# Feed-forward products of a streaming encoder on one core: a step's 512-column products ahead of its 256-column ones, operands laid at other places in SBUF

## The chip, the cores and the metric

One core of one Trainium2 chip runs the kernel. The metric is the device time of one execution in microseconds (us). Three runs of the kernel before lie between 1232.41 and 1232.6 us, with a median of 1232.55 us.

## What is computed

The reference is a two-layer encoder on 256 tokens of width 1024. Each layer is a half-step feed-forward (SwiGLU of width 2816), a mixer of three branches with one input and one output projection, a cross-attention to 256 memory tokens, and a second half-step feed-forward. The part that the change touches:

```python
def swiglu(h, w1, w3, w2):
    return (jax.nn.silu(h @ w1) * (h @ w3)) @ w2

for l in range(DEPTH):                                   # DEPTH = 2
    x = x + 0.5 * swiglu(rms_norm(x, ffn1_norm_g[l]), ffn1_w1[l], ffn1_w3[l], ffn1_w2[l])
    ...                                                  # mixer, cross-attention
    x = x + 0.5 * swiglu(rms_norm(x, ffn2_norm_g[l]), ffn2_w1[l], ffn2_w3[l], ffn2_w2[l])
return rms_norm(x, final_norm_g)
```

All arrays are float32. D_MODEL is 1024 (8 blocks of 128, KD), D_FF is 2816 (22 blocks of 128, KF).

## The kernel before

**Two parts of every number.** TensorE multiplies in the type fp32r. Each float32 operand is held as a hi part, rounded to fp32r, and a lo part, what the rounding left. A product of two such operands is hi x hi + hi x lo + lo x hi. For the weights, ScalarE makes the hi part (`w_hi`, line 127) and VectorE the lo part (`w_lo`, line 128) from the float32 weights `w_raw`, which SP's DMA queue brings (line 100).

**Feed-forward.** The activations lie with features on the partitions: `xn` is the input, 8 blocks of 128 features, and `g` the hidden one, 22 blocks. For block k, `x[:, k]` is a [128, 2, 256] piece: the hi parts of 256 tokens and their lo parts. `mm_w` makes a block's share with two products. The first loads 128 columns of `w_hi` as the array's stationary weights and streams all 512 columns of `x[:, k]`, hi and lo, into a PSUM bank of 512 columns. The second loads the same slice of `w_lo` and streams the 256 hi columns alone into the bank's second half. So 512- and 256-column products alternate. `gemm_w` takes a *step* of weights from `W` (`W.take`): up to 4 blocks by 256 output columns, and works it into two banks (m = 0 and 1, 128 output columns each), 4 blocks each. For w1 and w3 a bank is two steps of 4; for w2 it is five steps of 4 and one of 2. `gemm_both` does the same for the very first 256 columns of w1 and w3 together, whose steps are shorter. ScalarE and VectorE then add a bank's halves (`f_p`, `f_t`), and make `g` of them.

The last feed-forward's w2 (`final`), and half of the mixer's input projection, go through `gemm_x`, where the roles are exchanged: the activations are the stationary operand and 512 columns of weights stream. The other projections go through `gemm_n`: three products of 256 columns with weights as the stationary operand.

**The order of work.** The Tile framework orders each engine's instructions from a simulated timeline and from priorities. Weights are split up to three steps ahead (`SPLIT_AHEAD`), into three buffers each of `w_hi` and `w_lo`; a buffer is free when the last product that reads it is done.

**Where the operands lie.** The tables `XN_AT`, `G_AT` and `W_AT` shift a tile's contents by a number of float32 elements (4 bytes each) inside a slightly larger tile. The built program places `xn`'s tile 64 bytes past a multiple of 256 bytes of a partition, `g`'s tile 160 bytes, and the `w_hi` and `w_lo` tiles 128 bytes, in both kernels. While one product streams, the weights of the next are loaded. In this text the *distance* of a product is the start of its streaming operand minus the start of the weights that are loaded meanwhile, modulo 256 bytes. In the kernel before it is, by these tables:

| Products | streaming operand at | weights loaded meanwhile at | distance |
|---|---|---|---|
| `gemm_w`, `xn` | 64 + 4x8 = 96 | 128 + 4x16 = 192 | 160 |
| `gemm_w`, `g` | 160 + 4x48 = 352, so 96 | 192 | 160 |
| `gemm_x` (weights stream), `xn` | 128 + 4x56 = 352, so 96 | 96 | 0 |
| `gemm_x`, last w2 with `g` | 128 + 4x48 = 320, so 64 | 160 + 4x40 = 320, so 64 | 0 |
| `gemm_n`, `xn` of mixer and attention | 96 | 128 + 4x48 = 320, so 64 | 32 |

All blocks and slices are multiples of 256 bytes apart, so a distance holds for all products of a kind.

Of the kernel before, what the change touches and what calls it, by code (L numbers as in the profile page):

```python
# [9 lines left out]
F32R = mybir.dt.float32r  # L10
# [5 lines left out]
P = 128  # L16
D = 1024
S = 256
KD = D // P
# [5 lines left out]
CW = 256  # L25
# [5 lines left out]
PART_BUFS = 3  # L31
# [2 lines left out]
QE_BUFS = 1  # L34
T3_BUFS = 8
PAD = {"xn": 16, "g": 128, "mix": 0}
XN_AT = {"ffn1": 8, "mix": 8, "xattn": 8, "ffn2": 8}

W_AT = {("w13", False): 16, ("w1", False): 16, ("w3", False): 16, ("w2", False): 16, ("w2", True): 48,
        ("in", True): 56, ("kv", False): 40, ("kv", True): 48, ("out", False): 0, ("o", False): 0, "other": 48}  # L40
G_AT = (48, 40)
MIX_AT = 0
Q_AT, P_AT = 56, 8
X_LOADS = ((0, 1), (1, 1), (2, 2), (4, 2), (6, 2))
# [18 lines left out]
class Weights:  # L63
# [45 lines left out]
    def _split(self):  # L109
        nc, i = self.nc, self.n_split  # L110
        self.n_split += 1
        u, unit, at, nk = self.steps[i]
        while self.n_load < len(self.pieces) and self.pieces[self.n_load][0] <= u:
            self._load()
        at_ = W_AT.get((unit.key, unit.beside), W_AT["other"])
        hi = self.pool.tile([P, 4 * CW + 64], F32R, name="w_hi", tag="w_hi", bufs=PART_BUFS)[:, at_:at_ + 4 * CW]
        lo = self.pool.tile([P, 4 * CW + 64], F32R, name="w_lo", tag="w_lo", bufs=PART_BUFS)[:, at_:at_ + 4 * CW]
        if unit.key == "w13":
            hi, lo = (t[:, 0:2 * nk * CW].rearrange("p (h k c) -> p h k c", h=2, k=nk) for t in (hi, lo))
            t = self._both(u, at).rearrange("p (h k c) -> p h k c", h=2, k=nk)  # L120
        elif unit.beside:
            hi, lo = (t.rearrange("p (h k c) -> p h k c", h=2, k=2)[:, :, 0:nk, :] for t in (hi, lo))
            t = self.raw[u].rearrange("p h (k c) -> p h k c", k=4)[:, :, at:at + nk, :]
        else:
            hi, lo = (t.rearrange("p (k c) -> p k c", k=4)[:, 0:nk, :] for t in (hi, lo))
            t = self.raw[u].rearrange("p h (k c) -> p h k c", k=4)[:, at, 0:nk, :]
        self.last = nc.scalar.copy(hi, t)  # L127
        nc.vector.tensor_tensor(out=lo, in0=t, in1=hi.bitcast(F32), op=ALU.subtract)  # L128
        self.parts[i] = (hi, lo)
# [88 lines left out]
def trunk(ctx: ExitStack, tc: tile.TileContext, a: dict, out: bass.AP, stop=None, dbg=None):  # L218
# [9 lines left out]
    class Bank:  # L228
# [28 lines left out]
            self.mm(acc, lh, rl, False, False)  # L257
            self.mm(acc, ll, rh, False, stop)

        def mm_w(self, wh, wl, x, begin, stop):  # L260

            self.mm(self.ap, wh, x, begin, stop)
            self.mm(self.ap[:, 1, :], wl, x[:, 0, :], False, stop)

    class Act:

# [22 lines left out]

    def placed(pool, name, k, at, **kw):  # L290

        n = k * 2 * S
        return pool.tile([P, n + PAD[name]], F32R, name=name, bufs=1, **kw)[:, at:at + n].rearrange(
            "p (k u s) -> p k u s", k=k, u=2)

    def mm_bank(split=None):
        return Bank("mm", split)
# [31 lines left out]
    vec_off, n = {}, 0  # L329
# [36 lines left out]
    def gemm_w(key, nk, x, banks):  # L366

        k0 = 0
        while k0 < nk:
            wh, wl, n = W.take(key)  # L370
            for m, bank in enumerate(banks):
                for k in range(n):
                    sl = slice(m * P, (m + 1) * P)
                    bank.mm_w(wh[:, k, sl], wl[:, k, sl], x[:, k0 + k], k0 + k == 0, k0 + k == nk - 1)
            k0 += n
            yield

    def gemm_both(x, pairs):

        k0 = 0  # L380
        while k0 < KD:
            wh, wl, n = W.take("w13")
            for u, banks in enumerate(pairs):
                for m, bank in enumerate(banks):
                    for k in range(n):
                        sl = slice(m * P, (m + 1) * P)
                        bank.mm_w(wh[:, u, k, sl], wl[:, u, k, sl], x[:, k0 + k], k0 + k == 0, k0 + k == KD - 1)
            k0 += n

    def gemm_x(key, nk, x, banks):  # L390
# [36 lines left out]
    class Norm:  # L427


        def __init__(self, l, name, mem=False):  # L430
            self.gains = col(l, name)
            if not mem:
                self.x = placed(keep, "xn", KD, XN_AT[name.split("_")[0]], tag="xn")
            self.ssq = small.tile([P, S], F32, name="ssq", tag="ssq", bufs=2)
# [38 lines left out]
    def ffn(l, f, nrm, nxt, last=False, setup=None):  # L473
        with tc.tile_pool(name="ffn", bufs=2) as fp:
            g = placed(fp, "g", KF, G_AT[last])
            if setup is not None:
                setup = setup(fp)

            for c in range(0, KF, 2):
                t = [fp.tile([P, 2, S], F32, name="f_t", bufs=3) for _ in range(2)]  # L480
                both = l == c == 0 and f == "ffn1"
                if both:
                    pairs = [[mm_bank(2) for _ in range(2)] for _ in range(2)]
                    gemm_both(nrm.x, pairs)
                for u, key in enumerate(("w1", "w3")):
                    if both:
                        banks = pairs[u]
                    else:
                        banks = [mm_bank(2) for _ in range(2)]
                        run(gemm_w(key, KD, nrm.x, banks))  # L490
                    for m in range(2):

                        p = fp.tile([P, S], F32, name="f_p", bufs=3)
                        nc.scalar.copy(p, banks[m][:, 1, :])  # L494
                        nc.vector.tensor_tensor(out=t[m][:, u, :], in0=banks[m][:, 0, :], in1=p, op=ALU.add)  # L495
                if both:
                    first_norm()
                for m in range(2):
                    nc.vector.tensor_tensor(out=t[m], in0=t[m], in1=nrm.R[:, None, :].to_broadcast([P, 2, S]),  # L499
                                            op=ALU.mult)  # L500
                    s = fp.tile([P, S], F32, name="f_s", bufs=2)
                    act(SILU, out=s, in_=t[m][:, 0, :], func=AF.Silu)
                    nc.vector.tensor_tensor(out=s, in0=s, in1=t[m][:, 1, :], op=ALU.mult)
                    hi, lo = split(g[:, c + m, 0, :], g[:, c + m, 1, :], s)
                if setup is not None:

                    with tc.issue_after(hi.ins), tc.issue_after(lo.ins):
                        next(setup, None)
# [3 lines left out]
            for c in range(0, KD, 2):  # L512
                banks = [mm_bank(2) for _ in range(2)]
                run(gemm_w("w2", KF, g, banks))
                for m in range(2):
                    add_tile(c + m, [banks[m][:, u, :] for u in range(2)], 0.5, nxt)
# [183 lines left out]
    def mixer(l, nrm, nxt, mp, kvp):  # L700
        R, rc = nrm.R, nrm.rc
        mix = placed(mp, "mix", KD, MIX_AT)

        def tokens_out(tok, j, gain):
# [472 lines left out]
    for l in range(DEPTH):  # L1177
# [6 lines left out]
        with tc.tile_pool(name="kvp", bufs=1) as kvp, tc.tile_pool(name="mix", bufs=T4_BUFS) as mp:  # L1184
            nxt = Norm(l, "xattn_norm_g")
            k = mixer(l, nrm, nxt, mp, kvp)
# [104 lines left out]
```

## Time and profile before

| What | Value |
|---|---|
| Median of three runs | 1232.55 us |
| Profiled execution, its own time | 1232.48 us |
| Its span, first to last instruction | 1230.7 us |
| TensorE busy (matmuls) | 1221.3 us, 99% of the span |
| VectorE, ScalarE busy | 936.0 us (76%), 738.1 us (60%) |
[...]

Of the profiled execution's 1232.48 us, 1.78 us lie outside the span. Matmuls are pipelined, so the duration of one overlaps the next, and a busy TensorE says little: what counts is the time from the start of one product to the start of the next, called its *pitch* here. It is read from the start times of the timeline, which prints hundredths of a microsecond and merges equal instructions that follow each other into one row with their count.

### The profile page before, as it was taken

How to read it: one execution, taken by the hardware profiler on the slowest of the kernel's cores; microseconds unless marked ns; L12 is line 12 of the kernel's file. 1: busy time of each engine (PE TensorE's matmuls, PEld its weight loads, DVE VectorE, ACT ScalarE, POOL GpSimd, SP SyncE). 2: the span in 40 equal slices, each digit the busy share in tenths (PEclk: the TensorE clock that was granted, in tenths of full speed). 3: DMA queues.
4: the chain of work that ended last, by engine and by line, in shares of the span. 5: the costliest groups of instructions: out<-in, count | busy, mean ns of one | idle time of the engine just before them, and what ended most of it. 6: DMA issues, size and time to landing. Idle time of an engine off the chain costs nothing.

```text
span 1230.7 us, 21670 instructions
## 1 busy us (share of the span) xinstructions
PE 1221.3 (99%) x8378; PEld 1101.4 (89%) x8378; DVE 936.0 (76%) x1649; ACT 738.1 (60%) x1309; POOL 30.5 (2%) x54
## 2 busy tenths in 40 slices
PE   9999999999999999999999999999999999999997
PEld 8888889988999988888888888899898999888886
DVE  7989866888777687776678886679787767778754
ACT  6666645556765665664466654465677646656643
POOL 1000000000100000000000000000000000000000
PEclk9999999999999999999999999999999999999999
DMA  7645555443344355455555455544433534555453
GB/s 264 242 181 192 174 189 200 146 163 138 137 173 171 123 185 201 176 205 188 189 216 204 177 200 188 189 171 158 153 138 145 197 138 155 193 184 200 177 188 120
DMA packets 62569, 219.32 MB, mean 178 GB/s; under 512 B 6913, under 2 KB 8193, under 8 KB 62209
## 3 DMA queue, kind: packets, MB, share of 16 engines
q1 hardware_dynamic: 60976, 213.35, 47.6%
q0 software_dynamic: 768, 3.86, 0.8%
q8 instruction: 66, 1.08, 0.3%
q10 hardware_dynamic: 720, 0.72, 0.2%
q14 instruction: 39, 0.31, 0.1%
HBM read 216.85 MB, written 1.05 MB: 177 GB/s over the span
## 4 chain that ended last, share of the span: by engine, by line
PE 95%; DVE 2%; ACT 1%; issue 1%; DMA 0%; POOLq 0%; POOL 0%; SPq 0%; DVEq 0%; ACTq 0%
PE mm L244 88%; PE aux L244 2%; PE aux L834 1%; DVE w_lo L128 0%; PE aux L832 0%; DMA w_raw<-in_weights_dram 0%; ACT w_hi L127 0%; PE mm L242 0%; PE aux L242 0%; PE aux L827 0%; PE aux L984 0%; PE aux L913 0%; PE aux L1105 0%; PE aux L970 0%; DVE qe L815 0%
## 5 line engine op out<-in xcount | busy, mean ns | idle before, releaser
L128 DVE TENSOR_TENSOR w_lo<-w_raw,w_hi 128x1024 fp32r<-128x1024 f32 (+1 forms) x411 | 494.3, 1205 | 212.5 <-ACT w_hi L127 207.4
L127 ACT CAST w_hi<-w_raw 128x1024 fp32r<-128x1024 f32 (+1 forms) x411 | 425.0, 1035 | 361.0 <-PE mm L244 219.3
L244 PE MATMUL mm<-xn,w_hi 128*128 128x512 f32 (+1 forms) x2028 | 601.2, 359 | 0.6 <-DVE xn L362 0.5
L244 PE MATMUL mm<-xn,w_lo 128*128 128x256 f32 x1728 | 476.7, 280 | 0.0
L244 PEld LDWEIGHTS mm<-xn,w_hi 128*128 128x128 f32 x2028 | 357.7, 188 | 56.3 <-DVE xn L362 0.7
L244 PEld LDWEIGHTS mm<-xn,w_lo 128*128 128x128 f32 x1728 | 324.6, 188 | 3.6
L244 PE MATMUL mm<-g,w_hi 128*128 128x512 f32 x528 | 180.8, 392 | 0.0
L244 PE MATMUL mm<-g,w_lo 128*128 128x256 f32 x528 | 141.8, 280 | 0.0
L244 PEld LDWEIGHTS mm<-g,w_hi 128*128 128x128 f32 x528 | 96.5, 188 | 19.0
L244 PEld LDWEIGHTS mm<-g,w_lo 128*128 128x128 f32 x528 | 99.3, 188 | 2.9
L244 PE MATMUL mm<-w_hi,xn 128*128 128x512 f32 (+1 forms) x318 | 89.1, 374 | 0.0
L494 ACT COPY f_p<-mm 128x256 f32<-128x256 f32 x176 | 63.9, 365 | 24.5 <-PE mm L244 23.8
L495 DVE TENSOR_TENSOR f_t<-mm,f_p 128x256 f32<-128x256 f32 x176 | 73.0, 418 | 2.5 <-ACT f_p L494 2.4
L244 PEld LDWEIGHTS mm<-w_hi,xn 128*128 128x128 f32 x318 | 57.2, 188 | 9.2
L499 DVE TENSOR_TENSOR f_t<-f_t,R 128x512 f32<-128x512 f32 x88 | 60.2, 688 | 1.9 <-ACT R L463 0.7
L244 PE MATMUL mm<-w_lo,xn 128*128 128x512 f32 (+1 forms) x160 | 56.6, 378 | 1.0 <-DVE w_lo L128 1.0
L244 PE MATMUL mm<-w_hi,g 128*128 128x512 f32 x176 | 51.9, 390 | 0.0
L244 PE MATMUL mm<-mem_n,w_hi 128*128 128x256 f32 x248 | 46.7, 284 | 0.0
L244 PE MATMUL mm<-o,w_hi 128*128 128x256 f32 x248 | 46.2, 281 | 0.0
L467 DVE SCALAR_TENSOR_TENSOR xT<-mm,xT 128x256 f32<-128x256 f32 x80 | 32.0, 419 | 17.3 <-PE mm L244 17.3
L244 PE MATMUL mm<-mix,w_hi 128*128 128x256 f32 x256 | 44.7, 279 | 0.0
L244 PE MATMUL mm<-w_hi,mem_n 128*128 128x512 f32 x128 | 39.5, 393 | 0.0
(253 smaller groups left out, 1476.6 us busy)
## 6 DMA issues: line engine op xcount, KB each, us to landing
w_raw<-in_weights_dram SPq DMA_DIRECT2D x395, 512.0 KB, 4.0
w_raw<-in_weights_dram SPq DMA_DIRECT2D x18, 256.0 KB, 3.6
m_t<-in_mem_t_dram POOLq DMA_DIRECT2D x2, 1024.0 KB, 6.4
xT<-in_x_t_dram SPq DMA_DIRECT2D x3, 256.0 KB, 6.0
cst<-in_c_cst_dram POOLq DMA_DIRECT2D x1, 696.0 KB, 4.5
out_dram<-yg SPq DMA_DIRECT2D x2, 320.0 KB, 2.5
gw<-in_gates_w_dram POOLq DMA_DIRECT2D x2, 256.0 KB, 6.8
fg<-in_final_norm_g_dram POOLq DMA_DIRECT2D x1, 512.0 KB, 5.7
```

Source lines behind the costliest of these rows:

```text
L127: self.last = nc.scalar.copy(hi, t)
L128: nc.vector.tensor_tensor(out=lo, in0=t, in1=hi.bitcast(F32), op=ALU.subtract)
L244: i = self.last = nc.tensor.matmul(acc, lhsT, rhs, start=begin, stop=stop, skip_group_check=True)
L467: nc.vector.scalar_tensor_tensor(out=xT[:, j, :], in0=h, scalar=scale, in1=xT[:, j, :], op0=ALU.mult, op1=ALU.add)
L494: nc.scalar.copy(p, banks[m][:, 1, :])
L495: nc.vector.tensor_tensor(out=t[m][:, u, :], in0=banks[m][:, 0, :], in1=p, op=ALU.add)
L499: nc.vector.tensor_tensor(out=t[m], in0=t[m], in1=nrm.R[:, None, :].to_broadcast([P, 2, S]), op=ALU.mult)
L834: nc.tensor.matmul(sb[bs, i, :], ke[:, 1 + i, cb], qe[:, 1 + i, cb], start=True, stop=True, skip_group_check=True)
```

## The change

Four things change, all in the feed-forward:

- `xn` and `g` hold all hi parts of all blocks, then all lo parts. A block's 512 columns are then two pieces of 256, 8 KB apart in `xn` and 22 KB apart in `g`.
- `mm_w` gets a whole step's products for a bank, and issues the 512-column ones of all its blocks first, then the 256-column ones.
- `XN_AT` and `G_AT` put `xn` at 64 and `g` at 64 (modulo 256 bytes). `W_AT` has one place for hi and one for lo weights: hi at 64, lo at 32. The distance is 0 while hi weights are loaded and 32 while lo weights are loaded.
- The mixer, the attention and the last w2 keep their places, and their order of products.

```diff
-XN_AT = {"ffn1": 8, "mix": 8, "xattn": 8, "ffn2": 8}
-
-W_AT = {("w13", False): 16, ("w1", False): 16, ("w3", False): 16, ("w2", False): 16, ("w2", True): 48,
...
-G_AT = (48, 40)
+XN_AT = {"ffn1": 0, "mix": 8, "xattn": 8, "ffn2": 0}
+
+W_FF = (48, 40)
+W_AT = {("w13", False): W_FF, ("w1", False): W_FF, ("w3", False): W_FF, ("w2", False): W_FF, ("w2", True): (48, 48),
...
+G_AT = (40, 40)
...
-        def mm_w(self, wh, wl, x, begin, stop):
-
-            self.mm(self.ap, wh, x, begin, stop)
-            self.mm(self.ap[:, 1, :], wl, x[:, 0, :], False, stop)
+        def mm_w(self, steps):
+
+
+            for wh, _, x, begin, stop in steps:
+                self.mm(self.ap, wh, x, begin, stop)
+            for _, wl, x, _, stop in steps:
+                self.mm(self.ap[:, 1, :], wl, x[:, 0, :], False, stop)
...
-        return pool.tile([P, n + PAD[name]], F32R, name=name, bufs=1, **kw)[:, at:at + n].rearrange(
-            "p (k u s) -> p k u s", k=k, u=2)
+        t = pool.tile([P, n + PAD[name]], F32R, name=name, bufs=1, **kw)[:, at:at + n]
+        return t.rearrange("p (k u s) -> p k u s" if name == "mix" else "p (u k s) -> p k u s", k=k, u=2)
...
             for m, bank in enumerate(banks):
-                for k in range(n):
-                    sl = slice(m * P, (m + 1) * P)
-                    bank.mm_w(wh[:, k, sl], wl[:, k, sl], x[:, k0 + k], k0 + k == 0, k0 + k == nk - 1)
+                sl = slice(m * P, (m + 1) * P)
+                bank.mm_w([(wh[:, k, sl], wl[:, k, sl], x[:, k0 + k], k0 + k == 0, k0 + k == nk - 1)
+                           for k in range(n)])
```

What this does to TensorE's order is seen in the first layer's first feed-forward, at w1's and w3's second 256 columns. `mm_372` and `mm_373` are the two banks; the numbers behind `w_hi` and `w_lo` tell one step from the next. Before, at the change from one step to the next:

```order
L244 MATMUL mm_373<-xn_126,w_hi_326 128x512
L244 MATMUL mm_373<-xn_126,w_lo_327 128x256
L244 MATMUL mm_372<-xn_126,w_hi_346 128x512
L244 MATMUL mm_373<-xn_126,w_hi_346 128x512
L244 MATMUL mm_372<-xn_126,w_lo_347 128x256
L244 MATMUL mm_372<-xn_126,w_hi_346 128x512
```

Now, over the same two steps:

```order
L246 MATMUL mm_373<-xn_126,w_hi_326 128x512 x4
L246 MATMUL mm_373<-xn_126,w_lo_327 128x256 x4
L246 MATMUL mm_372<-xn_126,w_hi_346 128x512 x4
L246 MATMUL mm_372<-xn_126,w_lo_347 128x256 x4
L246 MATMUL mm_373<-xn_126,w_hi_346 128x512 x4
L246 MATMUL mm_373<-xn_126,w_lo_347 128x256 x4
```

A hi and a lo product no longer take turns: four hi products follow each other, then four lo products, and a bank's share of a step has one change of kind in either direction instead of four. The scheduler sometimes mixes two banks. This is w2 of the same feed-forward, now, at the end of the first two banks (`mm_1606`, `mm_1607`) and the start of the next two (`mm_1741`, `mm_1742`):

```order
L246 MATMUL mm_1606<-g_161,w_hi_1674 128x512 x2
L246 MATMUL mm_1606<-g_161,w_lo_1675 128x256 x2
L246 MATMUL mm_1607<-g_161,w_hi_1674 128x512 x2
L246 MATMUL mm_1607<-g_161,w_lo_1675 128x256 x2
L246 MATMUL mm_1741<-g_161,w_hi_1697 128x512 x4
L246 MATMUL mm_1742<-g_161,w_hi_1697 128x512 x2
L246 MATMUL mm_1741<-g_161,w_lo_1698 128x256 x4
```

Here w2's last step of two blocks gives runs of two, and the next step's first run is six long, since two of the second bank's hi products come ahead of the first bank's lo products.

VectorE and ScalarE issue the same instructions in nearly the same order. SP's and POOL's orders are as before. This is VectorE in the same feed-forward, before, over one group of 256 hidden columns (`f_t` and `f_s` lead from the banks to `g`; `m_t` and `mem_n` belong to the attention's memory):

```order
L128 TENSOR_TENSOR w_lo<-w_raw,w_hi 128x1024
L495 TENSOR_TENSOR f_t<-mm,f_p 128x256
L503 TENSOR_TENSOR f_s<-f_s,f_t 128x256
L499 TENSOR_TENSOR f_t<-f_t,R 128x512
L128 TENSOR_TENSOR w_lo<-w_raw,w_hi 128x1024
L359 TENSOR_TENSOR g<-f_s,g 128x256
L495 TENSOR_TENSOR f_t<-mm,f_p 128x256
L503 TENSOR_TENSOR f_s<-f_s,f_t 128x256
L128 TENSOR_TENSOR w_lo<-w_raw,w_hi 128x1024
```

And now:

```order
L130 TENSOR_TENSOR w_lo<-w_raw,w_hi 128x1024
L501 TENSOR_TENSOR f_t<-mm,f_p 128x256
L509 TENSOR_TENSOR f_s<-f_s,f_t 128x256
L505 TENSOR_TENSOR f_t<-f_t,R 128x512
L130 TENSOR_TENSOR w_lo<-w_raw,w_hi 128x1024
L365 TENSOR_TENSOR g<-f_s,g 128x256
L509 TENSOR_TENSOR f_s<-f_s,f_t 128x256
L501 TENSOR_TENSOR f_t<-mm,f_p 128x256
L130 TENSOR_TENSOR w_lo<-w_raw,w_hi 128x1024
```

One `f_s` and one `f_t` have changed places; the lo weights stand where they stood.

## Rows read from the trace of the kernel before

**Rows 1.** The page: span, then each engine's busy us, share and instructions.

```profile
span 1230.7 us, 21670 instructions
PE 1221.3 (99%) x8378; PEld 1101.4 (89%) x8378; DVE 936.0 (76%) x1649; ACT 738.1 (60%) x1309; POOL 30.5 (2%) x54
```

**Rows 2.** The chain that ended last: shares by engine; one piece, start, us, products.

```profile
PE 95%; DVE 2%; ACT 1%; issue 1%; DMA 0%; POOLq 0%; POOL 0%; SPq 0%; DVEq 0%; ACTq 0%
...
450.86 175.55 PE mm L244 x1012
```

**Rows 3.** Matmuls by line and shape, whole span: count, busy us, mean ns, idle before.

```profile
L244 PE MATMUL mm<-xn,w_hi 128*128 128x512 f32 x1408 | 486.9, 393 | 0.6 <-DVE xn L362 0.5
L244 PE MATMUL mm<-g,w_hi 128*128 128x512 f32 x528 | 180.8, 392 | 0.0
```

**Rows 4.** Timeline of TensorE, first feed-forward: start us, us, instruction.

```profile
104.34 0.39 PE L244 MATMUL mm<-xn,w_hi 128*128 128x512 f32 x1
104.57 0.28 PE L244 MATMUL mm<-xn,w_lo 128*128 128x256 f32 x1
104.69 0.39 PE L244 MATMUL mm<-xn,w_hi 128*128 128x512 f32 x1
```

**Rows 5.** Timeline of TensorE in the last w2, 512 columns; first and last of a run.

```profile
1175.90 0.39 PE L244 MATMUL mm<-w_lo,g 128*128 128x512 f32 x1
...
1180.43 1.07 PE L244 MATMUL mm<-w_hi,g 128*128 128x512 f32 x4
```

**Rows 6.** Timeline of TensorE in w_out, 256 columns; first and last of a run.

```profile
352.78 0.39 PE L244 MATMUL mm<-mix,w_hi 128*128 128x256 f32 x2
...
355.93 0.28 PE L244 MATMUL mm<-mix,w_hi 128*128 128x256 f32 x1
```

**Rows 7.** Timeline of TensorE in the mixer, from 256 columns to 512.

```profile
216.14 0.28 PE L244 MATMUL mm<-xn,w_lo 128*128 128x256 f32 x1
216.25 0.63 PE L244 MATMUL mm<-w_hi,xn 128*128 128x512 f32 x2
216.72 0.39 PE L244 MATMUL mm<-w_lo,xn 128*128 128x512 f32 x1
216.95 0.63 PE L244 MATMUL mm<-w_hi,xn 128*128 128x512 f32 x2
```

**Rows 8.** The same, at a memory projection.

```profile
326.55 0.63 PE L244 MATMUL mm<-w_hi,mem_n 128*128 128x512 f32 x2
...
327.24 0.39 PE L244 MATMUL mm<-w_hi,mem_n 128*128 128x512 f32 x1
```

**Rows 9.** Timeline of TensorE in the mixer, from 512 columns to 256.

```profile
227.63 0.40 PE L244 MATMUL mm<-w_lo,xn 128*128 128x512 f32 x1
227.87 0.28 PE L244 MATMUL mm<-xn,w_lo 128*128 128x256 f32 x1
227.99 0.40 PE L244 MATMUL mm<-xn,w_hi 128*128 128x256 f32 x2
228.22 0.28 PE L244 MATMUL mm<-xn,w_lo 128*128 128x256 f32 x1
```

**Rows 10.** Timeline of TensorE at the start, four 512-column products of the feed-forward together.

```profile
10.43 1.09 PE L244 MATMUL mm<-xn,w_hi 128*128 128x512 f32 x4
11.36 0.28 PE L244 MATMUL mm<-xn,w_lo 128*128 128x256 f32 x1
```

**Rows 11.** Busy time by engine, 80 to 130 us: PE, PEld, DVE, ACT, POOL; clock, DMA.

```profile
80.00:130.00 50.00, 50.00 (x290) 44.02 (x289) 45.59 (x87) 34.74 (x65) 0.00 (x0) 1.00 0.52 186
```

**Rows 12.** Waits: TensorE over the whole span; then all from 80 to 130 us.

```profile
PE mm L244 <- DVE w_lo L128: 1.0, 2, 0.5
PE mm L244 <- DVE xn L362: 0.5, 1, 0.5
...
ACT w_hi L127 <- PE mm L244: 6.3, 8, 1.2
...
DVE w_lo L128 <- ACT w_hi L127: 4.4, 11, 0.7
```

More of the change, by code (lines that the diff above doesn't have):

```diff
@@ L36 @@
 PAD = {"xn": 16, "g": 128, "mix": 0}
-XN_AT = {"ffn1": 8, "mix": 8, "xattn": 8, "ffn2": 8}
-W_AT = {("w13", False): 16, ("w1", False): 16, ("w3", False): 16, ("w2", False): 16, ("w2", True): 48,
-        ("in", True): 56, ("kv", False): 40, ("kv", True): 48, ("out", False): 0, ("o", False): 0, "other": 48}
-G_AT = (48, 40)
+XN_AT = {"ffn1": 0, "mix": 8, "xattn": 8, "ffn2": 0}
+W_FF = (48, 40)
+W_AT = {("w13", False): W_FF, ("w1", False): W_FF, ("w3", False): W_FF, ("w2", False): W_FF, ("w2", True): (48, 48),
+        ("in", True): (56, 56), ("kv", False): (40, 40), ("kv", True): (48, 48), ("out", False): (0, 0),
+        ("o", False): (0, 0), "other": (48, 48)}
+G_AT = (40, 40)
 MIX_AT = 0
@@ L115, in _split @@
         at_ = W_AT.get((unit.key, unit.beside), W_AT["other"])
-        hi = self.pool.tile([P, 4 * CW + 64], F32R, name="w_hi", tag="w_hi", bufs=PART_BUFS)[:, at_:at_ + 4 * CW]
-        lo = self.pool.tile([P, 4 * CW + 64], F32R, name="w_lo", tag="w_lo", bufs=PART_BUFS)[:, at_:at_ + 4 * CW]
+        hi = self.pool.tile([P, 4 * CW + 64], F32R, name="w_hi", tag="w_hi", bufs=PART_BUFS)[:, at_[0]:at_[0] + 4 * CW]
+        lo = self.pool.tile([P, 4 * CW + 64], F32R, name="w_lo", tag="w_lo", bufs=PART_BUFS)[:, at_[1]:at_[1] + 4 * CW]
         if unit.key == "w13":
@@ L384, in gemm_both @@
                 for m, bank in enumerate(banks):
-                    for k in range(n):
-                        sl = slice(m * P, (m + 1) * P)
-                        bank.mm_w(wh[:, u, k, sl], wl[:, u, k, sl], x[:, k0 + k], k0 + k == 0, k0 + k == KD - 1)
+                    sl = slice(m * P, (m + 1) * P)
+                    bank.mm_w([(wh[:, u, k, sl], wl[:, u, k, sl], x[:, k0 + k], k0 + k == 0, k0 + k == KD - 1)
+                               for k in range(n)])
             k0 += n
```

## The prediction, made before the changed kernel was run

> **What bounds the kernel now.** I read the page first. TensorE is busy for 99% of the span [rows 1], and the chain of waits that ended last runs through it for 95%, in pieces as long as 175.55 us with no other engine between [rows 2]. The next question is whether anybody makes TensorE wait. Its own waits name 1.0 us for `w_lo` and 0.5 us for `xn`, over the whole span [rows 12], so nearly nothing outside TensorE can be won back. VectorE is the nearest follower: in a feed-forward stretch it works 45.59 of 50 us [rows 11]. The time is therefore the number of products times their pitch, and the change leaves the number alone. It has to be judged by pitch.
>
> The feed-forwards hold 1408 + 528 = 1936 pairs of a 512- and a 256-column product [rows 3]. The long piece of the chain is 506 such pairs in 175.55 us: 0.3469 us a pair [rows 2]. The timeline splits it into 0.23 us from a hi product to the lo product behind it and 0.12 us from there to the next hi product [rows 4]. Four pairs, a bank's share of a step, take 4 x 0.3469 = 1.3876 us. [...]
>
> **The change part by part.** *Removed and added.* No instruction is removed or added; products, weight loads, transfers and splits stay as many and as large. What moves is which product follows which, and the distances.
>
> *The settled pitch at the new distances.* The kernel already runs both. In the last w2, 512 columns at distance 0: 20 products from 1175.90 to 1180.43 us, 0.2265 us each [rows 5]. That run also streams two pieces of 256 columns, so the second piece costs nothing visible. In w_out, 256 columns at distance 32: 27 products from 352.78 to 355.93 us, 0.1167 us each [rows 6]. If every product of the feed-forward had these pitches, four pairs would take 4 x (0.2265 + 0.1167) = 1.3728 us, 0.0148 us less than now.
>
> *The price of changing kind.* These runs are long. After the change a run is four products, and then the kind changes. The mixer shows such changes, and there the distances are the ones of the new kernel on both sides: its 512-column products have distance 0, its 256-column ones 32, the last 256 before a 512 has 0, and the last 512 before a 256 has 32. From 256 to 512 the first three products behind the change take 216.95 - 216.25 = 0.70 us [rows 7], or 327.24 - 326.55 = 0.69 us [rows 8]; there are six such changes, three of either kind, so I take 0.694 us. Three settled products would take 0.680 us. The last 256 ahead of the change takes 216.25 - 216.14 = 0.11 us [rows 7]. From 512 to 256, the last 512-column product takes 227.87 - 227.63 = 0.24 us, with 0.235 within the rounding, and the next three of 256 take 228.22 - 227.87 = 0.35 us [rows 9]; there are three changes of this kind at distance 32, all alike. So neither end of a run has the settled pitch: the first products are slower, and the last 512 is slower by 0.009 us.
>
> *The sum for four pairs.* 0.694 (first three of 512) + 0.235 (the fourth) + 0.352 (three of 256) + 0.1125 (the fourth) = 1.3935 us, against 1.3876 now: +0.0059 us. There are 1936 / 4 = 484 such groups: +2.9 us. I take this value, since it is made of products in exactly the new neighbourhoods, while the settled runs are not.
>
> *Its bounds.* Below: all products settled, -0.0148 x 484 = -7.2 us. Above: the nearest row for four grouped hi products of the feed-forward itself is at the start, at the old distance: 11.36 - 10.43 = 0.93 us for four [rows 10]. With 0.235 instead of a fourth of that for the last, and with the fourth 256-column product at the 0.1167 of a settled one, four pairs take 0.6975 + 0.235 + 0.352 + 0.1167 = 1.4012 us, +0.0136, or +6.6 us.
>
> [...]
>
> *The order of the other engines.* Costed at nothing. A step's first lo product now stands behind four hi products instead of one, so the lo weights are wanted 3 x 0.23 us later, and a `w_hi` buffer is done four lo products (0.47 us) ahead of the step's end, so ScalarE, whose largest wait in the stretch is for that buffer (6.3 us of 50), can start sooner, and VectorE behind it (4.4 us) too [rows 12]. The cover is VectorE's free 9%: 50 - 45.59 us [rows 11]. If it were gone, TensorE would run at VectorE's pace, which a change of 1% in pitch does not reach. A gain is bounded by the 1.5 us that TensorE waits today [rows 12]; the stall for `xn` stands in the first steps of one block each, whose order is the same, so I take none. SP's and POOL's queues are untouched. The order of `f_s` and `f_t` on VectorE shifts by one place, off the path.
>
> *The sum.* The profiled execution took 1232.48 us (span 1230.7), 0.07 under the median. 1232.48 + 2.9 = **1235.4 us**, 0.24% slower. About 0.2%, or 2.5 us, is what a measurement of this kernel can tell from no change.
>
> **The rivals.**
>
> *Faster: the short runs settle at once.* The place is the first and second 512-column product of every run in the feed-forward. A pattern that repeats 484 times may find a rhythm of its own, as the alternating pairs did. Fully settled it gives 1232.48 - 7.2 = 1225.3 us. With only the 0.235 at each run's end kept, four pairs take 1.3728 + 0.0085 = 1.3813, and the time is 1229.4 us. For it: the settled rows [rows 5, 6] are long and steady. Against: in the mixer no run settled with its first product [rows 7, 8]. It decides when the changes of kind cost less than 0.0097 us per four pairs (the 0.0148 gained less the 0.0051 that 2.5 us are).
>
> *No change: gain and price cancel.* If a run settles with the second product, as one of 0.232 us and then 0.2265, four pairs take 0.232 + 2 x 0.2265 + 0.235 + 0.352 + 0.1125 = 1.3845, -1.5 us: 1231.0 us. If the distances have no effect of their own and a pair of any order takes what it takes now, it is 1232.5 us. The half of the mixer's changes with 0.69 us [rows 8] are near this. [...]
>
> *More slowly than forecast.* Grouping itself is the harm, as at the start [rows 10]: up to 1232.48 + 6.6 = 1239.1 us. It belongs to the side of my forecast.
>
> That the change does not do what it says is excluded by the order: the runs of four are there.
>
> **How the numbers follow.** Slower, by the changes of kind: 0.44, within 1235 to 1239 us. No change: 0.33, between 1230.0 and 1235.0. Faster, settled runs: 0.23, from 1225.3 to 1230. My sum lies just past the bound between slower and no change, hence the small margin between the two. The range holds 8 in 10 when it leaves out the fastest tenth and the slowest tenth: the first tenth is fully settled runs below 1228.0, and the last lies above 1238.0, where grouping costs nearly as much as at the start. The slower case alone: 1235 to 1238.
>
> **What would show each step.** In the changed kernel's timeline, a run of four 512-column and four 256-column products in a feed-forward should take 1.39 to 1.40 us from one group's first start to the next. The first three of 512 should take 0.69 to 0.70 us, the last 0.24, and the 256-column ones 0.46 to 0.47 together. The mixer, the attention and the last w2 should be as before, and the clock 1.00. TensorE's waits should stay under 2.5 us, and ScalarE's wait for `w_hi` buffers should shrink. The prediction is wrong if a group takes under 1.383 us: then the short runs settle. It is wrong above too if a group takes over 1.40 us, or if waits for `w_lo` appear in TensorE's list.

## The result, and the profile after

The changed kernel takes 1242.47 us (median of four runs, 1242.28 to 1242.65) against 1232.57 in the same comparison: 1.008 times as long, 95% interval 1.0069 to 1.0092. That is 9.9 us slower where 2.9 were forecast, and above the range's 1238. The sign was right, but the miss of 7.0 us is larger than the forecast itself.

The page after, span and engines, answers to [rows 1]:

```profile
span 1240.7 us, 21657 instructions
PE 1230.2 (99%) x8378; PEld 1100.8 (89%) x8378; DVE 936.9 (76%) x1649; ACT 741.5 (60%) x1309; POOL 32.3 (3%) x54
```

The span is 10.0 us longer, and TensorE is busy for 99% of it again. Its whole list of waits (us in total, times, longest), beside [rows 12]:

```profile
PE mm L246 <- DVE xn L360: 1.0, 1, 1.0
PE aux L331 <- DVE mhalf L333: 1.0, 1, 1.0
PE mm L246 <- DVE w_lo L130: 1.0, 2, 0.5
PE mm L246 <- DVE xn L368: 0.7, 1, 0.7
```

`w_lo` costs the same 1.0 us, and `xn` 1.7 us instead of 0.5: at most 1.2 us of the 10. (The list adds up to 3.7 us, over the 2.5 us that the prediction allowed; the list before comes to 2.5.) The rest has to be in the pitch. The longest piece of the chain that ended last, its start, us and products, after, beside [rows 2]:

```profile
454.06 177.74 PE mm L246 x1008
```

A pair of a 512- and a 256-column product takes 177.74 / 504 = 0.3527 us instead of 0.3469. Here is one bank's share of a step after the change, four products of 512 columns and four of 256. Each row of the timeline merges the equal products that run at one moment, so neighbouring rows can share a product (x2); what counts are the starts.

```profile
106.90 0.40 PE L246 MATMUL mm<-xn,w_hi 128*128 128x512 f32 x1
107.14 0.63 PE L246 MATMUL mm<-xn,w_hi 128*128 128x512 f32 x2
107.38 0.63 PE L246 MATMUL mm<-xn,w_hi 128*128 128x512 f32 x2
107.61 0.39 PE L246 MATMUL mm<-xn,w_hi 128*128 128x512 f32 x1
107.85 0.28 PE L246 MATMUL mm<-xn,w_lo 128*128 128x256 f32 x1
108.32 0.40 PE L246 MATMUL mm<-xn,w_hi 128*128 128x512 f32 x1
```

The first 512-column product takes 0.24 us to the next start, and so on to 107.85; the four of 256 columns take 0.47, and the group 108.32 - 106.90 = 1.42. With the trace's start times in nanoseconds, over the 394 runs of four 512-column products: 241, 237, 233 and 231 ns; over the 439 runs of four 256-column ones: 472.7 ns together. So the group costs 1.4147 us on average. Over 484 groups that would be 13.1 us more than the 1.3876 us of before. It is less because 360 of the 1936 512-column products stand in runs of other lengths, and those take 232 ns on average instead of 235.2, waits left out. Over all pairs, also without waits, four pairs take 1.3881 us before and 1.4088 after: 10.0 us in 484 groups.

Nearly nothing else moved. The gaps from each feed-forward product's start to the next product's, added up over the trace, are 674.5 us before and 684.4 after: 9.9 of the span's 10.0 us, any waits in them included. For all other stretches 0.1 us are left. In the last w2, whose order and places were kept, 11 products of 512 columns take 1178.13 - 1175.64 = 2.49 us, 0.2264 each, as in [rows 5]:

```profile
1175.64 0.62 PE L246 MATMUL mm<-w_hi,g 128*128 128x512 f32 x2
...
1178.13 0.40 PE L246 MATMUL mm<-w_lo,g 128*128 128x512 f32 x1
```

The granted clock is the same too, 1.00 in the stretch below and 0.999 of full speed on average over either span. VectorE works less in a stretch of 50 us, 44.38 us instead of 45.59; so it does in e2 and e3 below (44.51 and 44.44), where TensorE is as slow. The stretch of [rows 11], and its first wait, beside [rows 12]:

```profile
80.00:130.00 50.00, 50.00 (x285) 43.23 (x285) 44.38 (x78) 34.54 (x64) 0.00 (x0) 1.00 0.49 180
```

```profile
ACT w_hi L129 <- PE mm L246: 9.8, 14, 1.0
```

### The profile page after: what moved, and what is told of

Its sections match the earlier page's. It is cut to its first block, busy times and chain, and to the rows that moved or that the text cites. A ratio compares the mean times of both kernels' runs of the same rounds, so it can differ in the third digit from the quotient of the medians.

```text
span 1240.7 us, 21657 instructions
## 1 busy us (share of the span) xinstructions
PE 1230.2 (99%) x8378; PEld 1100.8 (89%) x8378; DVE 936.9 (76%) x1649; ACT 741.5 (60%) x1309; POOL 32.3 (3%) x54
## 4 chain that ended last, share of the span: by engine, by line
PE 95%; DVE 3%; ACT 1%; issue 1%; DMA 0%; POOLq 0%; POOL 0%; SPq 0%; DVEq 0%; ACTq 0%
PE mm L246 87%; PE aux L246 2%; PE aux L840 1%; DVE w_lo L130 1%; DVE qe L821 0%; DMA w_raw<-in_weights_dram 0%; PE aux L838 0%; ACT w_hi L129 0%; PE mm L244 0%; DVE xc L915 0%; PE aux L244 0%; PE aux L833 0%; PE aux L990 0%; PE aux L919 0%; PE aux L1111 0%
## 5 line engine op out<-in xcount | busy, mean ns | idle before, releaser
L246 PE MATMUL mm<-xn,w_hi 128*128 128x512 f32 (+1 forms) x2028 | 502.5, 362 | 1.7 <-DVE xn L360 1.0
L246 PEld LDWEIGHTS mm<-xn,w_hi 128*128 128x128 f32 x2028 | 336.8, 188 | 38.1 <-ACT w_hi L129 1.2
L246 PE MATMUL mm<-xn,w_lo 128*128 128x256 f32 x1728 | 313.7, 281 | 0.0
L246 PEld LDWEIGHTS mm<-xn,w_lo 128*128 128x128 f32 x1728 | 275.5, 188 | 30.2
L246 PE MATMUL mm<-g,w_hi 128*128 128x512 f32 x528 | 145.5, 396 | 0.0
L246 PEld LDWEIGHTS mm<-g,w_hi 128*128 128x128 f32 x528 | 89.7, 188 | 12.2
L246 PEld LDWEIGHTS mm<-g,w_lo 128*128 128x128 f32 x528 | 81.3, 188 | 12.1
L246 PE MATMUL mm<-g,w_lo 128*128 128x256 f32 x528 | 84.0, 280 | 0.0
```

The source lines that it names most:

```text
L246: i = self.last = nc.tensor.matmul(acc, lhsT, rhs, start=begin, stop=stop, skip_group_check=True)
```

## The experiments

The kernel before took 1232.5 to 1232.7 us beside each of these kernels. "Grouped" is the new order (four 512-column products, then four of 256), "alternating" the old. Distances are given as 512-column / 256-column product.

| Kernel | order | distances | us | ratio, 95% interval |
|---|---|---|---|---|
| before | alternating | 160 / 160 | 1232.57 | 1 |
| after | grouped, 4 | 0 / 32 | 1242.47 | 1.0069 to 1.0092 |
| e1, layout alone | alternating | 160 / 160 | 1232.52 | 0.999 to 1.0008 |
| e2, order alone | grouped, 4 | 160 / 160 | 1242.31 | 1.0062 to 1.0092 |
| e3, places alone | alternating | 32 / 0 | 1242.81 | 1.0067 to 1.0097 |
| e4, order and places | grouped, 4 | 0 / 32 | 1242.54 | 1.0065 to 1.0098 |
| e7, runs of 8 | grouped, 8 | 0 / 32 | 1235.29 | 1.0011 to 1.0031 |
| e8, runs of 8, old places | grouped, 8 | 160 / 160 | 1241.95 | 1.0061 to 1.0091 |
| e9, runs of up to 16 | grouped, 16 | 0 / 32 | 1233.31 | 0.9997 to 1.0016 |
| e10, places swapped | alternating | 0 / 32 | 1229.45 | 0.9963 to 0.9983 |
| e11, one place | alternating | 0 / 0 | 1240.23 | 1.0047 to 1.0077 |
| e12, one place | grouped, 4 | 0 / 0 | 1238.55 | 1.0033 to 1.0067 |
| e13 | alternating | 0 / 160 | 1235.42 | 1.0014 to 1.0033 |
| e14 | alternating | 160 / 32 | 1234.21 | 1.0004 to 1.0024 |

Beware of one turn: the distance looks at the weights loaded *meanwhile*. When kinds alternate, a 512-column product runs while lo weights are loaded (in the kernel before, the product that starts at 104.34 us [rows 4] takes 0.39 us, and a load of lo weights, 0.19 us long, starts at 104.34 us too), so the change's own places give 32 / 0 in that order (e3), and 0 / 32 needs hi and lo weights at each other's place (e10). So what e3 loses is no part of the changed kernel's loss: its products have other distances. And except for the kernels at 160 / 160, `xn` and `g` lie at 64 throughout, so these runs don't tell the distance from the weights' own place, nor do they test the 256 bytes of the modulus.

### One part at a time

**e1_layout_alone**: the kernel before with the new layout only.

```diff
-            "p (k u s) -> p k u s", k=k, u=2)
+        return t.rearrange("p (k u s) -> p k u s" if name == "mix" else "p (u k s) -> p k u s", k=k, u=2)
```

> The kernel before with one part of the change: xn and g hold all hi parts, then all lo parts, so that a block's 512 columns are two pieces far apart. Order (hi and lo in turn) and distances (160) stay. Theory A (the price is paid at each change from lo to hi products and back, once products of a kind stand together; layout is free): a pair stays at 347 ns, the time at 1232.5 us. Rival B (the second, distant piece costs each 512-column product): in the changed kernel four pairs take 1413 ns, 26 more than before, so each 512-column product would pay 6.6 ns, a pair 353 ns, and the time would be 1232.5 + 1936 x 0.0066 = 1245 us, like the changed kernel's 1242.5 or above. Rival C (the new distances are the harm): 1232.5 us, as A.

1232.52 us. **e2_order_alone**: `mm_w` and `gemm_w` as in the change, layout and all places of before (`XN_AT` 8, `W_FF = (16, 16)`, `G_AT` 48).

```diff
-            self.mm(self.ap, wh, x, begin, stop)
-            self.mm(self.ap[:, 1, :], wl, x[:, 0, :], False, stop)
+            for wh, _, x, begin, stop in steps:
+                self.mm(self.ap, wh, x, begin, stop)
+            for _, wl, x, _, stop in steps:
+                self.mm(self.ap[:, 1, :], wl, x[:, 0, :], False, stop)
```

> The kernel before with one part of the change: a step's 512-column products first, then its 256-column ones. Layout and distances (160) stay. Theory A: four pairs take some 1413 ns as in the changed kernel, since the price is that of the order; 1242 us, at least above 1238. Rival B (layout) and rival C (distances): four pairs stay at 1387 ns, 1232.5 us. If order and distances only act together, 1232.5 us too, and the run of both parts has to tell.

1242.31 us. **e3_places_alone**: the new places only, layout and order of before.

```diff
-XN_AT = {"ffn1": 8, "mix": 8, "xattn": 8, "ffn2": 8}
+XN_AT = {"ffn1": 0, "mix": 8, "xattn": 8, "ffn2": 0}
+W_FF = (48, 40)
-G_AT = (48, 40)
+G_AT = (40, 40)
```

> The kernel before with one part of the change: the places of xn, g and the weights, so that a hi product has distance 32 (lo weights are loaded meanwhile) and a lo product has distance 0. Layout and order (hi and lo in turn) stay. Theory A: the alternating pairs keep a rhythm of their own, between 343 ns (if each has the settled 226.5 + 116.7) and 352 ns (if each hi product has the 235 ns of the last one of a run); middle 347, 1232.5 us within 3. Rival C (these distances are harmful with hi weights): a pair at 353 ns, 1245 us. Rival B: as A.

1242.81 us. **e4_order_places**: the changed kernel without the new layout (e1's diff taken back).

> The changed kernel with the layout of before: a block's hi and lo parts side by side, so that 512 columns are one piece. Theory S (the layout costs nothing in any order): as the changed kernel, 1242.4 us, with the same fall 241, 237, 233, 231 ns in a run of four. Rival L (the second piece, far away, starts each run badly): the fall is gone, and the time is near the 1235.4 of the prediction.

1242.54 us, with the same fall (241, 237, 233, 231 ns). So the layout is free in either order, and theory B, the distant second piece, falls, as L does. The order alone loses as much as the whole change, as theory A had it. The places alone do too, 10.3 us off theory A's 1232.5 and near rival C's 1245: the two losses don't add. The chain's long piece shows both, e2 first (504 pairs at 0.3527 us), then e3 (506 pairs at 0.3525):

```profile
454.00 177.78 PE mm L246 x1008
```

```profile
454.01 178.35 PE mm L246 x1012
```

The equal size hides two different patterns. In e2, at distance 160, there is no fall in a run of four: 233, 235, 233 and 235 ns on average, so all products are slow. In the changed kernel the run falls from 241 to 231 ns and ends there; longer runs show whether it would fall further.

### The length of a run

**e7_runs_of_8**: the changed kernel; both banks' hi products of a step, then both banks' lo products.

```diff
-            for m, bank in enumerate(banks):
-                bank.mm_w([(wh[:, k, sl], wl[:, k, sl], x[:, k0 + k], k0 + k == 0, k0 + k == nk - 1)
-                           for k in range(n)])
+            for bank, h, _, xk, begin, stop in steps:
+                bank.mm(bank.ap, h, xk, begin, stop)
+            for bank, _, lo, xk, _, stop in steps:
+                bank.mm(bank.ap[:, 1, :], lo, xk[:, 0, :], False, stop)
```

> The changed kernel with longer runs: the hi products of both banks of a step (8), then the lo products of both (8), so half as many changes of kind. Layout and distances as changed. Theory A (each run pays at its start: 241, 237, 233, 231 ns in the changed kernel, then settles at 227): eight hi products take some 1850 ns instead of 1885, eight pairs 2790 ns instead of 2827, and the feed-forwards 242 x 37 = 9 us less: 1233.5 us. If the products do not settle after the fourth but stay at 235, eight pairs stay at 2827 ns: 1242.5 us. Rival B (each 512-column product pays for its distant piece) and rival C (each pays for its distance): no change, 1242.5 us.

1235.29 us: 7 of the 10 us are back, though theory A's 1233.5 is missed by 1.8, and the 1242.5 of all others falls. The timeline of one group, and within its run the fourth product:

```profile
107.10 2.01 PE L246 MATMUL mm<-xn,w_hi 128*128 128x512 f32 x8
108.95 1.09 PE L246 MATMUL mm<-xn,w_lo 128*128 128x256 f32 x8
109.88 0.40 PE L246 MATMUL mm<-xn,w_hi 128*128 128x512 f32 x1
...
107.80 0.40 PE L246 MATMUL mm<-xn,w_hi 128*128 128x512 f32 x1
```

Three products take 107.80 - 107.10 = 0.70 us, all eight 1.85, and the eight of 256 columns 0.93. In nanoseconds the run goes 232, 236, 228, 233, 231, 227, 227, 235 (189 runs behind eight lo products): after five products it has settled, and the last is slower again.

**e8_runs_of_8_old_places**: e7's order at `XN_AT` 8, `W_FF = (16, 16)`, `G_AT` 48.

> The kernel before's places (distance 160 throughout), with the changed layout, and both banks of a step worked as eight 512-column products and then eight 256-column ones. Theory S (a place sets the level to which a run settles, a change of kind sets how far above it a run starts): at distance 160 grouped 512-column products stay at about 234 ns and 256-column ones at 118 to 119 ns whatever the length of the run, so longer runs win nothing: about 1241.5 us. Theory A (only the number of changes of kind counts): half the changes of the order alone, so half of its 9.7 us: about 1237.4 us, and runs that settle below 230 ns.

1241.95 us, as theory S had it; theory A, which counted changes of kind alone, falls by 4.5 us. The run of eight at distance 160 takes 110.03 - 108.17 = 1.86 us here, and over all 209 such runs it averages 233.8 ns a product, the last half no better than the first:

```profile
108.17 2.03 PE L246 MATMUL mm<-xn,w_hi 128*128 128x512 f32 x8
110.03 1.11 PE L246 MATMUL mm<-xn,w_lo 128*128 128x256 f32 x8
110.98 0.40 PE L246 MATMUL mm<-xn,w_hi 128*128 128x512 f32 x1
```

So once products are grouped, the new places are worth 6.7 us in runs of eight, and nothing in runs of four.

**e9_runs_of_16**: e7, with every second step begun by its lo products.

```diff
+            for part in ((0, 1) if turn % 2 == 0 else (1, 0)):
+                for bank, h, lo, xk, begin, stop in steps:
...
+            turn += 1
```

> The changed kernel, but a step's two banks are worked as eight 512-column products and eight 256-column ones, and every second step begins with its 256-column ones, so that up to 16 of a kind follow each other. Theory S: the first five 512-column products of a run are dear (with runs of 8: 233, 236, 229, 233, 230 ns) and the rest take 227, the 256-column ones 116.7: (1.850 + 8 x 0.227) / 16 + 0.1167 = 0.3459 us a pair against 0.3472 before, times 1936: 2.5 us under the kernel before, about 1230 us. Since the order breaks some runs into 12 and 4, 1230 to 1233. Rival W (lo weights are wanted too early): TensorE waits for w_lo or ScalarE for buffers, over 1234 us.

1233.31 us, not told apart from before. That is above the 1230 that full runs would give, and 0.3 past the 1233 allowed for broken ones: only 29 runs of 512-column products are 16 long; 82 are 12 and 82 are 4. One full run, its fourth product, and its end:

```profile
605.26 3.82 PE L246 MATMUL mm<-g,w_hi 128*128 128x512 f32 x16
608.92 2.03 PE L246 MATMUL mm<-g,w_lo 128*128 128x256 f32 x16
...
605.96 0.40 PE L246 MATMUL mm<-g,w_hi 128*128 128x512 f32 x1
608.68 0.40 PE L246 MATMUL mm<-g,w_hi 128*128 128x512 f32 x1
```

605.96 - 605.26 = 0.70 us for the first three, 608.92 - 608.68 = 0.24 for the last. From the sixth product to the one before the last they take 227 ns. TensorE waits 1.4 us for `w_lo` instead of 1.0, so rival W has 0.4 us of waits for them at most.

### Which distance it is

**e10_places_swapped**: e3, with hi weights at 32 and lo at 64 instead of the reverse.

```diff
-W_FF = (48, 40)
+W_FF = (40, 48)
```

> The kernel before's layout and alternating order, with xn and g at 64, hi weights at 32 and lo weights at 64 (modulo 256 bytes): a 512-column product then has distance 0 and a 256-column one distance 32, the pair of the long settled runs, while the kinds alternate. Theory D (the distance alone sets a product's pitch): 0.2265 + 0.1167 us a pair, 7 us faster than before, 1225 us. Theory S (every product behind a change of kind is dear, and here every product is): 0.241 + 0.118 us a pair, up to 1255 us. Rival N (alternation has its own rhythm, which the places do not set): within 2 us of 1232.5.

1229.45 us: 0.27% faster than the kernel before, and 1% faster than the changed one. It is the best of all kernels here. The four rows give 0.22 to 0.23 us behind a hi product's start and 0.12 behind a lo product's; the chain's long piece has 506 pairs at 0.3450 us:

```profile
109.28 0.28 PE L246 MATMUL mm<-xn,w_lo 128*128 128x256 f32 x1
109.40 0.39 PE L246 MATMUL mm<-xn,w_hi 128*128 128x512 f32 x1
109.62 0.28 PE L246 MATMUL mm<-xn,w_lo 128*128 128x256 f32 x1
109.74 0.39 PE L246 MATMUL mm<-xn,w_hi 128*128 128x512 f32 x1
```

```profile
450.80 174.55 PE mm L246 x1012
```

Theory D's 1225 is not reached (226.9 + 118.0 ns in the long piece, not 226.5 + 116.7). Theory S's "every product behind a change of kind is dear" falls: here all are behind one, and none is. Rival N is out by 1.1 us.

**e11_alternating_one_place** and **e12_grouped_one_place**: e3 and the changed kernel, with hi and lo weights both at 64.

```diff
-W_FF = (48, 40)
+W_FF = (48, 48)
```

> The kernel before's layout and alternating order, xn, g, hi and lo weights all at 64: every product has distance 0. Beside the same order with 0 for 512 columns and 32 for 256 (1229.45 us). Theory H (the distance of the 512-column products is what counts): 227.8 and 118.7 ns as there, 1229 to 1230 us. Rival P (the 256-column products have a price of their own at distance 0, 120.4 ns as where they had it behind 512-column ones at 32): 1.7 ns x 1936 more, about 1232.8 us.

> The changed kernel with the lo weights at the hi weights' place (64), so that every product of the feed-forward has distance 0, the one at a run's end too. Theory B (a run starts badly since the product before it has the other kind's distance): the fall 241, 237, 233, 231 ns is gone, 512-column products take 227 ns at once, and the time lies between 1225 and 1231 us, by what a 256-column product takes at distance 0 (0.113 to 0.120 us). Rival W (the change of width itself is what a run has to recover from): the fall stays, about 1242 us.

e11 takes 1240.23 us, and both its theories fall: the 512-column products have the same distance 0 as in e10, yet take 235.1 ns in the long piece instead of 226.9. The rows show them at 0.24, 0.24, 0.23 in turn, a pattern of three pairs that repeats:

```profile
106.14 0.40 PE L246 MATMUL mm<-xn,w_hi 128*128 128x512 f32 x1
106.38 0.28 PE L246 MATMUL mm<-xn,w_lo 128*128 128x256 f32 x1
106.50 0.40 PE L246 MATMUL mm<-xn,w_hi 128*128 128x512 f32 x1
106.74 0.28 PE L246 MATMUL mm<-xn,w_lo 128*128 128x256 f32 x1
106.86 0.40 PE L246 MATMUL mm<-xn,w_hi 128*128 128x512 f32 x1
107.09 0.28 PE L246 MATMUL mm<-xn,w_lo 128*128 128x256 f32 x1
```

e12 takes 1238.55 us, between its theories: the four 512-column products take 930 ns instead of 942, the 256-column ones 475.5 instead of 472.7. So the other kind's distance at a run's end can be a part of the price at most (3.9 us, which also hold what distance 0 does to the 256-column products). Nor does rival W hold, a fixed price for the change of width: where every distance is 0, grouping in fours is 1.7 us *faster* than alternating (e11 to e12). At 160 / 160 it costs 9.7 us (before to e2), and at 0 / 32 it costs 13.1 (e10 to e4). What an order costs depends on the distances, even in its sign.

**e13_512_at_0_alone** and **e14_256_at_32_alone** split e10 in two: first hi weights at 160 and lo at 64, then hi at 32 and lo at 160.

```diff
-W_FF = (40, 48)
+W_FF = (8, 48)
...
+W_FF = (40, 8)
```

> The kernel before's layout and alternating order; only the distance of the 512-column products goes from 160 to 0, that of the 256-column ones stays 160. With the run below it tells which half of the swapped places' gain (distances 0 and 32, 1229.45 us) is whose. Theory M (each distance has a price of its own, and prices add): by the swapped places' 227.8 ns against 230.0, 2.2 ns x 1936 = 4.3 us faster than before, 1228.3 us. Rival I (only the pair of distances has a pitch, as 0 and 0 gave 235.2 ns for the same 512-column products): over 3 us away from that, most likely above 1231 us.

> The kernel before's layout and alternating order; only the distance of the 256-column products goes from 160 to 32, that of the 512-column ones stays 160. Theory M (prices add): 118.7 ns against 118.0, 0.7 ns x 1936 = 1.4 us slower than before, 1234.0 us. Rival I (only the pair has a pitch): over 3 us away from that, on either side.

1235.42 and 1234.21 us. Theory M fits e14 (1234.0) and misses e13 by 7.1 us, where rival I holds. Each half alone is slower than before, by 2.9 and 1.7 us; together they are 3.1 us faster. The prices of two distances don't add: the pair has a pitch, not the product. The chain's long pieces, e13 and e14, 506 pairs each, at 0.3491 and 0.3478 us:

```profile
451.43 176.63 PE mm L246 x1012
```

```profile
451.76 176.00 PE mm L246 x1012
```

## Why the prediction was right in sign and wrong in size

*What bounds the kernel* held. The time is products times pitch before and after: the starts of the feed-forward's products account for 9.9 of the 10.0 us. In no experiment do the waits that TensorE's list names add up to more than 4.1 us, against 2.5 before.

*The settled pitches* held: 227 ns in the middle of e9's runs, and 117 ns in its runs of fifteen 256-column products.

*The price of changing kind* held where runs are long. In e9's full runs the first three products take 696.7 ns (21 runs between full ones), and the last 235.0: the prediction's 0.694 and 0.235 us. In e7, 189 runs behind eight lo products take 696.6.

*The sum for four pairs* is the step that failed. It took these prices over "in exactly the new neighbourhoods", that is, the neighbours were alike one product back. The terms measured in runs of four, and what the sum had:

| Term | predicted, us | measured, us |
|---|---|---|
| first three of 512 columns | 0.694 | 0.711 |
| the fourth | 0.235 | 0.231 |
| four of 256 columns | 0.4645 | 0.4727 |
| sum | 1.3935 | 1.4147 |

The largest term of the miss is the first three products, 0.017 of 0.021 us. Seen another way, the sum holds a gain of 7.2 us from the new distances, against 10.0 us for the changes of kind. But e2, grouped at the old distances, and the changed kernel differ by 0.2 us: in runs of four the gain isn't there. Also, the distance 32 that the prediction gives w_out's products [rows 6] stands in no table, since none places `mix`; the 117 ns of e9's runs, at 32 by the tables, agree with it.

Four of the six mixer changes that the prediction averaged stand behind 12 or 86 products of 256 columns. The other two, at 226.03 and 833.44 us, stand behind two only, and cost the same 0.690 and 0.697 us. This is the second of them, before:

```profile
832.52 0.85 PE L244 MATMUL mm<-w_hi,xn 128*128 128x512 f32 x3
833.21 0.40 PE L244 MATMUL mm<-xn,w_hi 128*128 128x256 f32 x2
833.44 0.40 PE L244 MATMUL mm<-w_lo,xn 128*128 128x512 f32 x1
833.67 0.62 PE L244 MATMUL mm<-w_hi,xn 128*128 128x512 f32 x2
834.13 0.40 PE L244 MATMUL mm<-w_lo,xn 128*128 128x512 f32 x1
```

In e7 two histories exist side by side: 16 runs of four behind eight lo products take 696.6 ns for their first three, as the runs of eight do, while 21 runs of four behind four lo products take 707.1. In the changed kernel, 375 runs behind four take 710.8, and the nine behind eight 696.7. So more than the products on either side of a change sets its price. It is no simple rule of the length of the run ahead: beside the mixer's two, in e9, 14 runs of four behind four lo products take 695.9. What else sets the price was not found out, and stays open.

*The upper bound* failed with it: 1.4012 us was built from [rows 10] for the first three products and from the mixer for the rest. Those rows' own 0.93 us for four was close to the truth, 0.942, but the bound took 0.9325 and then 0.352 + 0.1167 = 0.4687 for the 256-column ones, which took 0.4727. The nearest rival was "grouping itself is the harm", 1239.1 us; at these distances it is what happened, at 3.4 us more.

*The rivals.* "The short runs settle at once" did not happen in the changed order. It did for another kernel: alternating products at distances 0 and 32 (e10) run at 0.3450 us a pair, four pairs at 1.380, about the case that the prediction priced at 1.3813. "Gain and price cancel" came true only with runs of up to 16 (e9).

*The other engines, costed at nothing*: `w_lo` made nobody wait more. The stalls for `xn`, left out of the sum, grew by 1.2 us, of which the span can show little beside the pitch. ScalarE's wait for `w_hi` buffers was to shrink and grew, from 6.3 to 9.8 us in the stretch. The order does that, and not the slower pitch: the wait is 9.7 us in e2, with the new order, and 6.6 in e3, as slow in the old one. TensorE's list shows no cost of it.

## What to carry to other kernels

This kernel, which TensorE fills to 99%, took from 1229.45 us (e10) to 1242.81 us (e3) with the same products, 1% apart. Its pitch went with the order of widths (before to e2, 9.7 us slower), the length of runs (the changed kernel to e7, 7.2 us faster), and the SBUF offsets of the operands (e3 to e10, 13.4 us faster). The price read in one neighbourhood, the mixer's 0.694 us for a run's first three products, was met in e9's full runs (0.697) and missed in the changed kernel's runs of four (0.711). So an edit of order or offsets wants a try of the period itself, and the two must be tried together: each half of the best pair of offsets was slower alone, by 2.9 and 1.7 us. Sum up the starts of a whole period. The mean duration of the 512-column products on `xn` moved by the same 5 ns (393 to 398) as the mean pitch of all 1936 (230 to 235), but durations overlap, and only starts add up to a time.

## What was not expected of the hardware

With the same products in the same order, only the offsets of `w_hi` and `w_lo` exchanged (e3 and e10), the time goes from 1242.81 to 1229.45 us: 13.4 us. A pair takes 0.3525 and 0.3450 us in the long pieces of the two chains. By what the offsets act, the runs don't show.

At a mean granted clock of 0.998 or 0.999 in every profiled run, 512-column products were seen at about 227 (e10), 230 (before), 235 (e11) and 241 ns (the first of four, after), each of them in patterns that repeat. In the changed kernel a group of four and four takes 1413 or 1414 ns in 350 of 389 cases, so the slow pattern is a rhythm, not scatter.
